# One decoder layer in fp32: the token mixer's weight loads issued from GpSimd's queue, and one statistics tile in another pool

## The chip, the cores and the metric

The kernel runs on one core of one Trainium2 chip. Its time is the device time of one execution in microseconds (us); lower is better. Times of several runs are given by their median. A profile is one execution recorded by the hardware profiler.

Short names used below: PE is TensorE (matmuls), PEld its weight loads, DVE VectorE, ACT ScalarE, POOL GpSimd, SP SyncE. SPq and POOLq are the sequencers of SP and POOL, which issue DMAs in the order of their programs.

## What is computed

One layer of a hybrid decoder on x of 2048 tokens by 1024 channels, in fp32: a token mixer and a gated feed-forward network, each on a modulated input and each followed by a LayerNorm.

```
u = x * (1 + scale) + shift                 # scale, shift, gate: rows of c @ w_ada
qa, ka, va, qb, kb, vb, ga, gb = split(u @ w_in)
ya = banded_attention(qa, ka, va, window 128, sinks)
yb = mixture of three dilated attentions (stride 1, 4, 16), merged by their denominators
y  = sigmoid(ga) * (ya @ w_a) + sigmoid(gb) * (yb @ w_b)
x  = LayerNorm(alpha * x + gate * (y @ w_o))
h  = silu(u2 @ w_gate) * (u2 @ w_up)         # u2: x modulated again
out = LayerNorm(alpha * x + gate2 * (h @ w_down))
```

## The kernel before

**Products.** Every fp32 operand of a large product is split into a high part and a rest (hi by ACT at L121, lo = src - hi by DVE at L122), and each product is three passes of matmuls over the parts: hi*hi, hi*lo, lo*hi.

**Weights.** `weights()` (L124) brings in one unit of weights of the token mixer: a tile `raw` of 128 x 1024 from the pool `raws` (3 buffers), one to four DMAs into it (L133), and the split into a tile `whl` (pool of 4 buffers), which PE reads. A DMA into a raw tile waits until the split of the tile that had this buffer before is done. The same pool of raw tiles serves the loads of `w_ada` in `ada_steps` (L197), which go on in the background. A unit has 24 matmuls of 512 columns on PE, one of the output stage (`w_a` and `w_b`, 768 columns) 18.

**Stages** (us from the start of the profile of before):
- 0 to 57, start-up: four groups of column pairs of `w_ada` (tile `pair`, L163) and of x (tile `xs`, L437), and four units of w_in (L431), are loaded by SP. DVE multiplies and adds the pairs (L172, L174) into `adc`, PE sums over the partitions (L183), DVE makes the scale and shift `mod` (L189), ACT the modulated input `ub` (L476) and its high part `ut`, and PE the first products (L418). PE, DVE and ACT follow an order written out by hand there. Of the four units' tiles three are the buffers of `raws`.
- 57 to 385: the dilated attention of stride 4 and 16, four residue classes; 385 to 823: four chunks of 512 tokens with the windowed attention and stride 1. The probabilities are transposed by DMA from SP (`pt`, L296) before the product with v. In both, the next stage's input is loaded by SP ahead (`xs`, L221; `ub`, L378).
- 823 to 1474: merging and output projection, chunks in the order 3, 0, 1, 2. `y_rows` (L900) loads each block of 128 tokens: `yl` (L908), `sty` (statistics, L909) and `xr` (L910); DVE and ACT make the merging weights (DVE L913 to L931, the exponentials on ACT at L917 and L932); PE transposes the merged rows (L953). ACT's sigmoids of the last gates ahead of it (L749) are stored to `s_s` (L750) and fetched later as `sg` (L990).
- 1474 to the end: gate and up with half of the multiplications of one level of Strassen (PE L1168), down (PE L1372), LayerNorms. `first_norm` (L1110) is here.

**What sets the order.** PE's order is that of the code (a manual schedule). On the other engines the order of instructions is set at compile time by a scheduler, by priorities: `weights()` has its priority raised by `PREFETCH` (100), so that its loads stand well ahead of their use. At run time every engine runs its program in order and waits on semaphores; an instruction that waits holds all that stands behind it on its engine, DMA issues on SPq and POOLq among them. Nothing reorders a queue at run time.

POOL has little to do before: three tables of distances (L251), casts of k (L605), an inverse square root per block (L772) and four stores of the normed input (`n_s`, L1049).

Of the kernel before, what the change touches and what calls it, by code (L numbers as in the profile page):

```python
# [12 lines left out]
F32 = mybir.dt.float32  # L13
# [44 lines left out]
def trunk(ctx, tc, x, c, w_ada, b_ada, w_in, sinks, w_a, w_b, w_o, ln1_g, ln1_b,  # L58
          w_gate, w_up, w_down, ln2_g, ln2_b, out):
    nc = tc.nc  # L60

    def dr(src, off, ap):
        return bass.AP(tensor=src.tensor, offset=src.offset + off, ap=ap)
# [56 lines left out]
    def split(hi, lo, src):  # L120
        nc.scalar.activation(hi, src, AF.Copy)  # L121
        nc.vector.tensor_tensor(lo, src, hi.bitcast(F32), op=OP.subtract)  # L122

    def weights(pieces, n=1024, by=None, offset=PREFETCH, into=None):  # L124


        with tc.high_priority(offset=offset):
            raw = raws.tile([128, 1024], F32, name="raw")
            o = 0
            for p in pieces:  # L130
                ap, m = p[:2]
                dst = p[2](raw) if len(p) > 2 else raw[:, o:o + m]
                nc.sync.dma_start(dst, ap)  # L133
                o += m
            whl = None if into else whls.tile([128, 2, 1024], F32R, name="whl")
            if by is not None:
                nc.vector.tensor_tensor(raw, raw, by, op=OP.mult)
            for i, (hi, lo) in enumerate(into or ()):
                split(hi, lo, raw[:, i * 512:(i + 1) * 512])
            if into is None:  # L140
                split(whl[:, 0, :n], whl[:, 1, :n], raw[:, :n])
        return whl
# [254 lines left out]
    def gate(us, c0):  # L397

        whl = weights([unit(c0)])
        ps = psum.tile([128, 512], F32, name="mm")  # L400
        dense(ps, KT, wT(whl), lambda k, b: us[k][b])
        return ps
# [4 lines left out]
    with ExitStack() as ph:  # L407
# [85 lines left out]
        def pool(name, bufs, stack=ph):  # L493
            return stack.enter_context(tc.tile_pool(name=name, bufs=bufs, reuse_waits="tile"))
# [46 lines left out]
        def project(us, pieces, outs, order, ps=None):  # L541
            if later is not None and ps is None:
                next(later, None)
            if ps is None:
                whl = weights(pieces)
                ps = psum.tile([128, 512], F32, name="mm")
                dense(ps, KT, wT(whl), lambda k, b: us[k][b])
            if order == 3:
                src = ps.rearrange("p (i a) -> p a i", a=4)
                hi, lo = (t.rearrange("p (a i) -> p a i", a=4) for t in outs)  # L550
            else:
                src, (hi, lo) = ps, outs
            with tc.high_priority(offset=EVICT):
                split(hi, lo, src)
            if nxt is not None:
                nxt.ahead(2)
            at.tick(5.2)

        def project_v(us, pieces_of, n, kper, lhs_of):
            ps = [psum.tile([128, 512], F32, name="mm") for _ in range(4)]  # L560
            for u0 in range(KT // kper):
                whl = weights(pieces_of(u0), kper * n)
                for t in range(4):
                    for kk in range(kper):
                        k = u0 * kper + kk
                        for i, (a, b) in enumerate(PASS):
                            nc.tensor.matmul(ps[t][:, :n], lhs_of(us[k][a], t),  # L567
                                             whl[:, b, kk * n:(kk + 1) * n],
                                             start=k == 0 and i == 0,
                                             stop=k == KT - 1 and i == 2)  # L570
                    if t % 2:
                        at.tick(2 * kper * n * 3 / 2400)
            return ps
# [193 lines left out]
    def layer_norm(pool, y, st, g, b, stats_only=False):  # L767
        mv = pool.tile([128, 2], F32, name="mv")
        rs = pool.tile([128, 1], F32, name="rs")
        nc.vector.bn_aggr(mv, st)  # L770
        nc.vector.tensor_scalar(rs, mv[:, 1:2], EPS, None, op0=OP.add)
        nc.gpsimd.tensor_tensor(rs, rs, mhalf, op=OP.pow)  # L772
        if not stats_only:
            scale_add(y, mv, g, rs, b)
        return mv, rs
# [27 lines left out]
    def x1t():  # L803
        return gp.tile([128, 4, 512], F32, name="x1t")
# [82 lines left out]
    with ExitStack() as ph:  # L887
# [5 lines left out]
        tmp = pool("tmp3", 2, ph)  # L893
# [166 lines left out]
    with ExitStack() as ph:  # L1060
        pool = partial(tile_pool, tc)
        w8 = pool("w8", 4, ph)
        tmp = pool("tmp4", 5, ph)
# [4 lines left out]
        lnp = pool("lnp", 2, ph)  # L1068
# [41 lines left out]
        def first_norm(l1, b):  # L1110

            t = x1t().rearrange("p a n -> p (a n)").rearrange("p (b n) -> p b n", b=2)
            nc.sync.dma_start(t, dr(n_s, b * 128 * D, [[D, 128], [128 * D, 2], [1, D]]))
            for i in range(2):
                st = tmp.tile([128, 2, 6], F32, name="st", bufs=2)
                for h in range(2):
                    nc.vector.bn_stats(st[:, h], t[:, i, h * 512:(h + 1) * 512])
                layer_norm(lnp, t[:, i], st, l1[:, :D], l1[:, D:])
            nc.sync.dma_start(dr(x1_s, (1024 + b * 128) * D, [[D, 128], [128 * D, 2], [1, D]]), t)
# [198 lines left out]
        for n, (p, g, w) in enumerate(sets):  # L1318
# [10 lines left out]
            if n in (1, 2):  # L1329
                hook(then, 7, partial(first_norm, l1, 2 * n - 2))  # L1330
# [31 lines left out]
    with ExitStack() as ph:  # L1362
# [3 lines left out]
        tmp = pool("tmp5", 2, ph)  # L1366
# [144 lines left out]
```

## Time and profile before

| | |
|---|---|
| time, median of 3 runs | 2775.33 us (2774.93 to 2778.13) |
| time of the profiled execution | 2777.24 us |
| its span, first to last instruction | 2775.5 us |
| PE busy | 2701.5 us (97%) |
| DVE, ACT, POOL busy | 69%, 43%, 2% |
| DMA queues | q1 (hardware): 503.06 MB, 61.2% of 16 engines; q0 (software): 2.10 MB, 0.2% |
| mean granted TensorE clock | 0.991 |

The profiled execution took 1.74 us more than its span. PE is busy for all but 74 us of the span, so a change of the time shows either in the holes of PE or in its granted clock. Of the two queues the hardware one holds the DMAs that SP issues, and the software one those that POOL issues (the four stores of L1049).

### The profile page before, as it was taken

The numbers are of one execution on the slowest core, as the hardware profiler recorded it, in microseconds if no ns is written. First come the engines' busy times: TensorE is split into PE (matmuls) and PEld (weight loads), VectorE is DVE, ScalarE is ACT, GpSimd is POOL, SyncE is SP. The second block draws the span as 40 slices with busy tenths as digits, with TensorE's granted clock in tenths as the row PEclk, the third lists the DMA queues.
The fourth block names the chain that finished last, engine by engine and source line by source line (L and its number), as shares of the span: only waits on it lengthen the run. The fifth ranks groups of instructions, "written<-read, shape, count | busy, mean of one in ns | idle before, by whom it ended". The sixth has DMA issues, their size and how long they took to land.

```text
span 2775.5 us, 36388 instructions
## 1 busy us (share of the span) xinstructions
PE 2701.5 (97%) x13331; PEld 2215.2 (80%) x13331; DVE 1918.9 (69%) x3506; ACT 1199.6 (43%) x1984; POOL 57.2 (2%) x63
## 2 busy tenths in 40 slices
PE   7999999999998999999999999998999999999998
PEld 5778778887887888888887888886888888888886
DVE  7766677788768867756458878767886666333387
ACT  3555565666594444343343333324222232432353
POOL 0000000000000000000000000000000000000011
PEclk9999999999999999999999999999999999999999
DMA  9966867776788476573545557725672334654463
GB/s 287 238 178 166 198 148 167 151 177 140 163 202 276 154 243 190 184 209 108 175 151 187 208 203 281 265 86 191 227 267 78 114 110 150 203 176 142 145 235 141
DMA packets 581332, 507.48 MB, mean 183 GB/s; under 512 B 207192, under 2 KB 467360, under 8 KB 581152
## 3 DMA queue, kind: packets, MB, share of 16 engines
q1 hardware_dynamic: 580576, 503.06, 61.2%
q8 instruction: 104, 1.70, 0.3%
q0 software_dynamic: 576, 2.10, 0.2%
q14 instruction: 76, 0.62, 0.1%
HBM read 341.67 MB, written 127.48 MB: 169 GB/s over the span
## 4 chain that ended last, share of the span: by engine, by line
PE 66%; DVE 4%; DMA 4%; ACT 1%; issue 1%; POOL 0%; SPq 0%; DVEq 0%; ACTq 0%; POOLq 0%
PE mm L1168 29%; PE mm L154 16%; PE acc L1372 14%; PE mm L1037 2%; PE o L1037 1%; PE s L1037 1%; PE o L306 1%; DMA x1t<-xT_s 1%; DMA x1t<-l_s 1%; PE s L271 1%; DMA sg<-s_s 1%; PE mm L567 1%; DVE cb L122 1%; DVE w L122 0%; ACT x1t L826 0%
## 5 line engine op out<-in xcount | busy, mean ns | idle before, releaser
L1168 PE MATMUL mm<-cb,w 128*128 128x512 f32 x3696 | 859.1, 394 | 9.9 <-ACT cb L121 3.2
L1168 PEld LDWEIGHTS mm<-cb,w 128*128 128x128 f32 x3696 | 693.8, 188 | 174.3 <-ACT w L121 5.4
L154 PE MATMUL mm<-ut,whl 128*128 128x512 f32 x3072 | 733.9, 395 | 10.1 <-DVE ut L122 5.1
L154 PEld LDWEIGHTS mm<-ut,whl 128*128 128x128 f32 x3072 | 572.2, 189 | 140.3 <-DVE ut L122 10.9
L1372 PE MATMUL acc<-hw 128*128 128x512 f32 x1848 | 419.1, 389 | 0.0
L1372 PEld LDWEIGHTS acc<-hw 128*128 128x128 f32 x1848 | 347.0, 188 | 71.9
L122 DVE TENSOR_TENSOR whl<-raw,whl 128x1024 fp32r<-128x1024 f32 (+1 forms) x228 | 265.2, 1164 | 145.8 <-ACT whl L121 145.6
L121 ACT ACTIVATE whl<-raw 128x1024 fp32r<-128x1024 f32 (+1 forms) x228 | 230.1, 1010 | 294.5 <-issue 69.0
L121 ACT ACTIVATE w<-g 128x1024 fp32r<-128x1024 f32 (+1 forms) x176 | 166.8, 951 | 387.6 <-PE mm L1168 318.7
L122 DVE TENSOR_TENSOR hw<-raw,hw 128x1536 fp32r<-128x1536 f32 x77 | 135.2, 1757 | 171.5 <-ACT hw L121 170.6
L121 ACT ACTIVATE hw<-raw 128x1536 fp32r<-128x1536 f32 x77 | 114.7, 1490 | 241.7 <-PE acc L1372 209.6
L122 DVE TENSOR_TENSOR w<-g,w 128x1024 fp32r<-128x1024 f32 (+1 forms) x176 | 191.1, 1087 | 39.2 <-ACT w L121 37.7
L294 DVE TENSOR_TENSOR ehl<-te,ehl 128x512 f16<-128x512 f32 (+1 forms) x160 | 98.3, 615 | 114.6 <-ACT ehl L293 114.4
L567 PE MATMUL mm<-whl,ut 128*128 128x512 f32 (+1 forms) x768 | 160.3, 365 | 0.0
L567 PEld LDWEIGHTS mm<-whl,ut 128*128 128x128 f32 x768 | 137.4, 188 | 16.4
L154 PE MATMUL mm<-q,whl 128*128 128x512 f32 x576 | 137.3, 393 | 0.8 <-DVE q L122 0.4
L154 PEld LDWEIGHTS mm<-q,whl 128*128 128x128 f32 x576 | 109.0, 190 | 24.9 <-DVE q L122 0.8
L1172 DVE TENSOR_TENSOR t<-mm,t 128x512 f32<-128x512 f32 x138 | 94.6, 687 | 48.5 <-PE mm L1168 48.0
L283 DVE CUSTOM_DVE_ANT_0 te<-s,tab 128x256 f32<-128x256 f32 (+1 forms) x320 | 109.6, 381 | 2.2 <-PE s L271 2.0
L306 PE MATMUL o<-v,pt 128*128 128x192 bf16 x1096 | 92.4, 236 | 4.8 <-DMA pt<-ehl 4.6
L306 PEld LDWEIGHTS <-pt 128*128 128x128 f16 x1096 | 75.6, 99 | 25.4 <-issue 18.3
L293 ACT ACTIVATE ehl<-te 128x512 f16<-128x512 f32 (+1 forms) x160 | 89.7, 561 | 12.0 <-DMA pt<-ehl 9.8
(195 smaller groups left out, 2606.5 us busy)
## 6 DMA issues: line engine op xcount, KB each, us to landing
raw<-in_w_in_dram SPq DMA_DIRECT2D x132, 512.0 KB, 4.3
raw<-h_s SPq DMA_DIRECT2D x77, 512.0 KB, 3.9
g<-in_w_gate_dram SPq DMA_DIRECT2D x22, 1024.0 KB, 5.3
g<-in_w_up_dram SPq DMA_DIRECT2D x22, 1024.0 KB, 5.3
h_s<-g SPq DMA_DIRECT2D x22, 1024.0 KB, 5.6
t_s<-x1t SPq DMA_DIRECT2D x22, 1024.0 KB, 5.1
raw<-t_s SPq DMA_DIRECT2D x77, 256.0 KB, 4.0
h_s<-g SPq DMA_DIRECT2D x22, 768.0 KB, 5.3
```

Of the source, the lines that this page charges most:

```text
L121: nc.scalar.activation(hi, src, AF.Copy)
L122: nc.vector.tensor_tensor(lo, src, hi.bitcast(F32), op=OP.subtract)
L154: nc.tensor.matmul(ps, lhs(k, a), rhs(k, b), start=i == 0, stop=i == n - 1)
L283: nc.vector.tensor_tensor_reduce(out=te[:, h, :nk], in0=ps[h], in1=tables[h][:, 256 - nk:], scale=1.0, scalar=-3e38, op0=OP.add, op1=OP.ma ...
L293: nc.scalar.activation(eh[:, 0], te[:, :, :nk], AF.Copy)
L294: nc.vector.tensor_tensor(eh[:, 1], te[:, :, :nk], eh[:, 0], op=OP.subtract)
L306: nc.tensor.matmul(pv[:, h, a:], pt[:, (a * 2 + h) * nb + j], v[:, :3 - a], start=j == 0 and a == 0, stop=j == nb - 1 and a == 1)
L567: nc.tensor.matmul(ps[t][:, :n], lhs_of(us[k][a], t), whl[:, b, kk * n:(kk + 1) * n], start=k == 0 and i == 0, stop=k == KT - 1 and i == 2)
L1037: nc.tensor.matmul(pss[b], mT[k][a][:, b * 128:(b + 1) * 128], whl[:, bb, kk * 512:(kk + 1) * 512], start=k == 0 and i == 0, stop=k == KT ...
L1168: nc.tensor.matmul(ps, r.of(m, k, a), us[k][b][:, LEFT[m]], start=first and k == 0 and i == 0, stop=last and k == 3 and i == 2, skip_group ...
L1172: nc.vector.tensor_tensor(out, ps, other, op=op)
L1372: nc.tensor.matmul(ps, hw[:, a, t * 128:(t + 1) * 128], hw[:, b, 1024:], start=first and i == 0, stop=last and i == 2, skip_group_check=True)
```

## The change

One line in `weights()` makes POOL issue the loads of the mixer's weights (w_in behind the first four units, w_a, w_b, w_o) instead of SP; what is loaded, into which buffers, stays. One line in `first_norm` takes its small tile `st` from the pool `lnp`, where it had been one of two buffers of the pool `tmp`.

```diff
@@ weights()
                 dst = p[2](raw) if len(p) > 2 else raw[:, o:o + m]
-                nc.sync.dma_start(dst, ap)
+                nc.gpsimd.dma_start(dst, ap)
                 o += m
@@ first_norm()
-                st = tmp.tile([128, 2, 6], F32, name="st", bufs=2)
+                st = lnp.tile([128, 2, 6], F32, name="st")
```

The programs of the engines show what this moves. First POOL, at the start of the program, before the change (L82 and L83 make the identity matrix; a row with xN is N instructions in succession):

```order
L82 MEMSET ident 128x128
L83 ISA
L83 AFFINE_SELECT ident<-ident 128x128
L251 IOTA ub 128x256 x3
L605 CAST k<-k 128x128 x18
L772 TENSOR_TENSOR rs<-rs,mhalf 128x1 x12
L1049 DMA n_s<-xr 128x1024 x4
```

And POOL at the same place with the change:

```order
L82 MEMSET ident 128x128
L83 ISA
L83 AFFINE_SELECT ident<-ident 128x128
L133 DMA raw<-in_w_in_dram 128x2x512 x3
L251 IOTA ub 128x256
L133 DMA raw<-in_w_in_dram 128x2x512
L133 DMA raw<-in_w_in_dram 128x8x128 x8
L133 DMA raw<-in_w_in_dram 128x2x512 x4
```

Three loads are now the first DMAs of POOL's program, with nothing ahead of them there but the identity matrix; all later loads, the casts of k and the square roots stand in one line behind them.

The same place on SP, as a difference; the rows of u_s (L480) are stores of the modulated input in the start-up, those of xs (L221) loads for the next stage:

```order
 L480 DMA u_s<-ub 128x512 x6
-L133 DMA raw<-in_w_in_dram 128x2x512 x2
+L221 DMA xs<-in_x_dram 128x4x128
 L480 DMA u_s<-ub 128x512
-L133 DMA raw<-in_w_in_dram 128x2x512
+L221 DMA xs<-in_x_dram 128x4x128
 L480 DMA u_s<-ub 128x512
```

Before, these first weight loads stood behind six of the eight stores, which wait for the start-up's results; on POOL they stand behind none of them.

The second place is SP between the attention and the output projection (855 to 863 us in the profile of before), where the blocks of chunk 0 are fetched for merging (sty, xr) and the gates stored (s_s). Before:

```order
L909 DMA sty<-st_s 128x40
L910 DMA xr<-o_s 128x512
L133 DMA raw<-in_w_a_dram 128x4x128
L133 DMA raw<-in_w_b_dram 128x2x128
L909 DMA sty<-st_s 128x40
L910 DMA xr<-o_s 128x512
L750 DMA s_s<-ub 128x512
L910 DMA xr<-o_s 128x512
L133 DMA raw<-in_w_a_dram 128x4x128
L133 DMA raw<-in_w_b_dram 128x2x128
L909 DMA sty<-st_s 128x40 x2
```

With the change:

```order
L750 DMA s_s<-ub 128x512
L910 DMA xr<-o_s 128x512
L909 DMA sty<-st_s 128x40
L750 DMA s_s<-ub 128x512
L909 DMA sty<-st_s 128x40 x2
L750 DMA s_s<-ub 128x512
L910 DMA xr<-o_s 128x512
L909 DMA sty<-st_s 128x40
L378 DMA ub<-u_s 128x4x128 x3
L750 DMA s_s<-ub 128x512
```

The loads of statistics stand behind the stores of gates only, no longer behind loads that wait for a weight buffer. ACT's program follows at this place: the last sigmoids of L749 alternate with one or two exponentials (L917, L932) where two sigmoids came in succession before, and ACT has 46 table loads in the whole program instead of 42, each where it passes between the two functions.

PE's program is the same but for one group of transposes in the first chunk of the output projection, and the instructions of gate, up and down stand in the same order on every engine.

## Rows read from the trace of the kernel before

**Rows 1.** The page: the span, and PE's busy time

```profile
span 2775.5 us, 36388 instructions
PE 2701.5 (97%) x13331; PEld 2215.2 (80%) x13331; DVE 1918.9 (69%) x3506; ACT 1199.6 (43%) x1984; POOL 57.2 (2%) x63
```

**Rows 2.** Waits of PE: line, released by; us in total, times, longest

```profile
PE mm L225 <- DMA xs<-in_x_dram: 10.0, 5, 3.8
...
PE mm L418 <- ACT ut L121: 7.0, 2, 3.7
...
PE o L306 <- DMA pt<-ehl: 4.6, 3, 1.7
...
PE mm L953 <- ACT ub L749: 3.1, 1, 3.1
```

**Rows 3.** Waits of SP's queue: the loads of weights, for their buffer

```profile
SPq L133 <- DVE whl L122: 276.4, 102, 7.2
```

**Rows 4.** Line L133: who waited for its transfers (us, times)

```profile
  ACT whl L121: 36.9, 16
```

**Rows 5.** Timeline in the attention: start, us, engine, line, operation [idle before]

```profile
189.50 5.79 PE L154 MATMUL mm<-ut,whl 128*128 128x512 f32 x24
...
331.61 0.38 SPq L133 DMA_DIRECT2D raw<-in_w_in_dram  x1
...
347.78 1.06 ACT L121 ACTIVATE whl<-raw 128x1024 fp32r<-128x1024 f32 x1 [5.04 <-PE mm L567]
```

**Rows 6.** Timeline of the start-up, all engines

```profile
19.69 1.23 DVE L122 TENSOR_TENSOR whl<-raw,whl 128x1024 fp32r<-128x1024 f32 x1 [0.26 <-ACT whl L121]
...
30.77 0.35 DVE L172 TENSOR_SCALAR adc<-pair,cols 128x256 f32<-128x256 f32 x1 [1.16 <-DMA pair<-in_w_ada_dram]
...
32.15 0.78 ACT L476 ACTIVATE ub<-s,mod 128x512 f32<-128x512 f32 x1 [10.22 <-DVE mod L189]
...
33.64 1.52 PE L418 MATMUL mm<-ut,whl 128*128 128x512 f32 x2 [3.67 <-ACT ut L121]
...
43.73 0.96 SPq L133 DMA_DIRECT2D raw<-in_w_in_dram  x2
```

**Rows 7.** Windows, start-up: busy time of each engine, PEclk, DMA share, GB/s

```profile
20.00:30.00 10.00, 9.54 (x39) 7.53 (x37) 9.26 (x20) 1.90 (x3) 0.00 (x0) 1.00 1.12 338
30.00:40.00 10.00, 6.36 (x22) 4.90 (x23) 8.71 (x23) 2.71 (x4) 0.00 (x0) 0.66 1.12 339
```

**Rows 8.** Timeline between attention and output projection, all engines

```profile
855.07 0.38 SPq L133 DMA_DIRECT2D raw<-in_w_a_dram  x1
856.05 0.46 SPq L909 DMA_DIRECT2D sty<-st_s  x1
...
859.58 0.17 DVE L913 TENSOR_TENSOR sm<-sty,nsk 128x8 f32<-128x8 f32 x1 [1.88 <-DMA sty<-st_s]
...
860.65 1.28 ACT L749 ACT_TABLE_LOAD   x1
...
862.60 0.66 PE L953 MATMUL mm<-ident,yl 128*128 128x128 f32 x4 [3.11 <-ACT ub L749]
864.96 1.12 PE L953 MATMUL mm<-ident,yl 128*128 128x128 f32 x4 [1.71 <-DVE q L122]
```

**Rows 9.** Windows, same columns as rows 7, of this place

```profile
858.00:874.00 16.00, 10.40 (x44) 7.92 (x43) 12.30 (x44) 8.38 (x16) 0.00 (x0) 0.79 0.92 298
```

**Rows 10.** Timeline of SP and PE around one wait for xs

```profile
186.12 0.40 SPq L133 DMA_DIRECT2D raw<-in_w_in_dram  x1
187.41 2.70 SPq L296 DMA_TRANSPOSE pt<-ehl  x2
...
192.97 0.44 SPq L221 DMA_DIRECT2D xs<-in_x_dram  x1
...
198.36 0.63 PE L225 MATMUL mm<-ident,xs 128*128 128x128 f32 x4 [2.64 <-DMA xs<-in_x_dram]
```

**Rows 11.** Line L1049, the DMAs that POOL issues: ns min/median/max, and landing

```profile
L1049 POOL DMA_DIRECT2D n_s<-xr x4: 533/536/746, 1472.2 to 1476.2; - x4
...
DMA to landing us min/median/max: 3.1/3.4/3.7
```

**Rows 12.** POOL's square roots: busy us, mean ns, idle before

```profile
L772 POOL TENSOR_TENSOR rs<-rs,mhalf 128x1 f32<-128x1 f32 x17 | 24.2, 1428 | 705.6 <-DVE rs L771 674.7 <-issue 30.7
```

## The prediction, made before the changed kernel ran

> **What bounds the kernel now.** I read the page first. PE is busy for 2701.5 of 2775.5 us [rows 1], so 74 us of holes, and the stretches at half clock that follow some of them, are all that a change of queues can win without shortening a matmul. Next I read PE's waits: who ended each hole [rows 2]. The reader is to look for the raw weights, or their split whl, and to miss them: PE's holes are put down to x tiles, modulated inputs, transposed probabilities and a sigmoid, of which no line is over 10.0 us. Third, SP's queue [rows 3]: there the loads of weights waited 276.4 us in 102 waits for a free buffer. That is large and looks like the prize, but it is the loads' own wait; it costs only what stands behind it on SP and is late for that reason. Fourth, the reverse: who waited for these loads [rows 4]: ACT, 36.9 us, and ACT is not full. In the attention a load issued at 331.61 is split at 347.78, three units later, and the split then waits for PE, not for the load [rows 5]. With 16 us of lead, an earlier load gives PE nothing. So the change must be judged at the few places where something else stood behind a weight load on SP, or where the loads now go at another time. The last views are timelines at the start-up and at the passage to the output projection, with windows for clock and DMA.
>
> **1. Start-up: three loads go out much earlier, +6.3.** Before, the first loads of L133 are issued at 43.73 [rows 6], behind the stores of the start-up. On POOL only the buffer holds them: the three raw tiles come free with the splits of the start-up's weights, of which the third begins at 19.69 and lasts 1.23, so all three are free by 20.9. From there 3 x 512 KB = 1.57 MB are moved in a stretch in which the DMA engines have no room: their share is 1.12 from 20 to 30 and from 30 to 40, at 338 and 339 GB/s [rows 7]. 1.57 MB at 339 GB/s are 4.6 us. What waits for DMA there is the path: DVE waits for a pair until 30.77, makes mod, ACT starts at 32.15 after 10.22 us without work, PE at 33.64 after 3.67 [rows 6]. DVE, ACT and PE keep a written order there, so nothing can be put in the hole. If the three loads delay the pair by their whole time, this hole grows by 4.6. The clock falls behind it already: 0.66 granted over 10 us is 6.8 us at the lower level (1.2 of 2.4 GHz), 3.4 us lost [rows 7]; a longer hole may lose half as much again, 1.7. Bounds: 0, if the pairs keep their rate, and 4.6 + 3.4 = 8.0 with a second whole stretch. I take +6.3, since rows 7 show no spare DMA time. Nothing is won back: after the start-up PE does not wait for weights.
>
> Here a rule speaks against the change. The rows show one stream of loads filling the DMA engines at 339 GB/s [rows 7]. The Trainium skill, page "DMA: Bandwidth & Descriptors", section "Issuing engines are not separate DMA queues", says that DMAs of SP, ACT and POOL run on the same 16 engines and interleave, and that issuing from several saves only issue time. By that rule the term is the +4.6 of shared bytes with its clock; if a second queue brought capacity of its own, it would be 0. No run here shows two queues at once.
>
> **2. Passage to the output projection, -4.0.** At 855.07 SP issues a weight load for which it had waited, and only at 856.05 the load of sty behind it; DVE gets sty at 859.58 after 1.88 us, ACT loads its table for the sigmoid at 860.65, behind the exponentials of that block, and PE goes on at 862.60 after 3.11 [rows 8]. With the change nothing that waits for a weight buffer stands ahead of sty; the stores of gates do, and they wait for sigmoids that PE feeds every 5.79 us [rows 5], which leaves a landing of some 3 us its time. So the hole of 3.11 can go. The next, 1.71 for DVE's part of q, belongs to the start of the stage and stays. Clock: 0.79 over 16 us is 6.7 us at the lower level, 3.4 lost [rows 9]; I count half, 1.7. Against that stand four more table loads on ACT, 1.28 each [rows 8], of which ACT's idle time takes most; I charge 0.8. Sum -3.1 - 1.7 + 0.8 = -4.0. Bounds: -6.5 (hole and whole clock loss gone) and +2.6 (two table loads on the path and the hole still there).
>
> **3. Attention: xs and pt, -1.5.** Typical is the hole at 198.36: its xs is issued at 192.97 behind two transposes of 2.70 us, and the weight load ahead of these, at 186.12, takes 0.40 [rows 10]. Taking out 0.4 at each of the three largest holes for xs gives -1.2, and 0.3 more for the three waits for pt. Bounds: -14.6, all of 10.0 and 4.6 [rows 2], if these transfers were late because they queued behind weights; +5, if the scheduler's new order of ACT and DVE opens as many holes as it closes.
>
> **4. POOL's queue, +0.5.** POOL now does all loads in order, and they wait for buffers. Behind them stand the casts of k and the square roots (1.43 us each [rows 12]). One of the latter is held for up to 2 us where the chunk's norm needs it; I charge 0.5, bounds 0 and 2. What a load costs POOL no row shows for these shapes. The nearest: a store of 128 rows of 4 KB takes 0.533 us and lands in 3.4 [rows 11]. A unit of w_in has 8 x 128 = 1024 rows of 512 B: between 0.533, if the cost is by instruction, and 8 x 0.533 = 4.3, if it is by row. PE takes 5.79 for a unit [rows 5], so both ends hide, at 16 us of lead. The shift of SP's own issue time (0.38 us each [rows 5]) frees SP, which is not the bound.
>
> **5. The tile st, 0.** Both pools have two buffers for it, the instructions are the same and nobody waits there.
>
> **Sum.** +6.3 - 4.0 - 1.5 + 0.5 = +1.3 on the profiled execution's 2777.24 gives 2778.5. That one lies 1.9 above the median of the runs, so I put the same +1.3 on 2775.33: 2776.6. A measurement of this kernel tells 0.2% (5.6 us) from no change.
>
> **Rivals.**
> *A, xs and pt were late because of the queue, faster.* In one queue a transfer waits for the 512 KB ahead of it. For it: SP's loads wait 276.4 us [rows 3], and xs and pt are small. Against it: in rows 10 the weight load is 6.8 us ahead of xs. If two thirds of the 14.6 go, term 3 is -9.7 and the whole +6.3 - 4.0 - 9.7 + 0.5 = -6.9: 2768.4. It decides from a term 3 of -8.4.
> *B, POOL's issue becomes the bound, slower.* If a row costs more than the 4.2 ns of rows 11 (0.533 over 128), a unit of 2048 rows (the windowed queries, 16 of them, two loads of 64 columns for 8 x 128 rows each) takes over 8.5 us where PE takes 5.79: 2.7 us each. Four in succession are 10.8, just under the lead of 16; at twice the price, 17 a unit, they are 45 less 16 = 29 per chunk, over four chunks 116. The point from which it decides is some 6.5 ns a row (13.3 - 5.79 = 7.5 a unit, four of them 30, less 16 = 14 per chunk). At that point 56 us are lost: 2832; a slight case, one chunk, gives about 2790. Against it: the one row of POOL's DMAs is far below.
> The Trainium skill, "SBUF — State Buffer", section "SBUF: two separate sides", warns that POOL cannot write descriptors while DVE runs certain fast copies. That would act as B does; no row here shows a DMA of POOL held in this way.
> *C, the start-up at its upper bound and no gain later, slower.* With term 1 at +8.0, term 2 at 0 and term 3 at 0, the sum is +8.5: 2783.8. For it: the written order, and that table loads are added just where term 2 expects its gain.
> *D, the loads are in effect unchanged.* If POOL's first loads are held up by POOL itself, term 1 is 0, and terms 2 to 4 give -5.0: 2770.3, within 0.2%. Against it: nothing stands ahead of them in POOL's program.
>
> **How the numbers follow.** My forecast, terms 1 to 4 near their values: 0.34, predicted time 2776.5, own range 2771 to 2781. D 0.10, which is counted half as no change and half as faster. A 0.20, C 0.24, B 0.12. Faster: A 0.20 and 0.05 of D, 0.25. Slower: B and C, 0.36. Same: 0.39. The range reaches down over most of A, to 2767, and up over C and the slight case of B, to 2791; outside are the far part of B (0.08), the bottom of A (0.06), and 0.04 for what I do not see.
>
> **What would show it.** Step 1: the hole of PE before L418 at some 38 instead of 33.64, the wait for a pair ahead of it longer than 1.16, the first loads of L133 at 17 to 21. Step 2: PE's wait for L749 gone from its list, sty issued right behind a store. Step 3: xs and pt still in the list with like sums. Step 4: casts and roots later but nobody waiting for them; L133's duration on POOL per load, which settles B. Wrong I would be if the pairs land as before although the DMA engines are full, if PE waits for whl, or if the new order on ACT and DVE opens holes of several us where the trace of before has none.

## The result, and the profile after

| | median | runs | ratio to the kernel before |
|---|---|---|---|
| before | 2775.13 us | 4 (2771.96 to 2778.13) | |
| changed | 2806.18 us | 4 (2803.07 to 2808.05) | 1.0104 [1.0091, 1.0117] |

The change costs 31 us; I had forecast no difference that can be told (2776.5, range 2767 to 2791). The profiled execution took 2808.05 us with a span of 2806.3. Its page, the lines that answer to rows 1, and the two DMA queues:

```profile
span 2806.3 us, 36596 instructions
PE 2706.8 (96%) x13331; PEld 2227.3 (79%) x13331; DVE 1923.7 (69%) x3506; ACT 1203.4 (43%) x1988; POOL 300.7 (11%) x383
...
q1 hardware_dynamic: 382944, 391.89, 46.2%
q0 software_dynamic: 32832, 113.27, 13.8%
```

POOL's software queue now moves 113 MB. PE is idle for 2806.3 - 2706.8 = 99.5 us, 25.5 more than before. Its waits, against rows 2 (line, released by; us in total, times, longest):

```profile
PE o L306 <- DMA pt<-ehl: 18.1, 11, 3.6
PE mm L225 <- DMA xs<-in_x_dram: 12.7, 6, 4.8
PE s L448 <- DMA xs<-in_x_dram: 12.2, 3, 8.4
PE mm L418 <- ACT ut L121: 6.6, 2, 3.4
...
PE mm L953 <- ACT ub L749: 2.7, 1, 2.7
...
PE mm L1037 <- ACT sg L992: 2.1, 2, 1.9
```

Rows 2 leave out one line of the kernel before, the second largest, which belongs beside these:

```profile
PE s L448 <- DMA xs<-in_x_dram: 8.5, 1, 8.5
```

The wait for the transposed probabilities has gone from 4.6 us to 18.1, those for xs (L225 and L448) grew by 6.4 together, and the wait for L749, which I had expected to go, is still 2.7. The first two are 19.9 of the 25.5. PE is also busy 5.3 us longer, although the group of L1168 alone takes 11.3 less (shown below): the matmuls elsewhere were slower, which the granted clock accounts for (see the attention, term 3). Between the first L567 and the first L953 of PE (60.5 and 897.4 in the changed kernel, 56.8 and 858.0 before, from the timelines) 35.7 us are lost; the start-up before it loses 3.7, and the output projection behind it takes 0.4 less than it had. Then something I had not looked for: gate and up take 8.1 us less (first L1168 to first L1372: 1513.7 to 2375.2, before 1474.7 to 2344.3).

### The profile page after: what moved, and what is told of

Same layout as the page of the kernel before. It is cut to its first block, busy times and chain, and to the rows that moved or that the text cites. A ratio compares the mean times of both kernels' runs of the same rounds, so it can differ in the third digit from the quotient of the medians.

```text
span 2806.3 us, 36596 instructions
## 1 busy us (share of the span) xinstructions
PE 2706.8 (96%) x13331; PEld 2227.3 (79%) x13331; DVE 1923.7 (69%) x3506; ACT 1203.4 (43%) x1988; POOL 300.7 (11%) x383
## 4 chain that ended last, share of the span: by engine, by line
PE 59%; DVE 7%; DMA 6%; issue 2%; ACT 2%; POOL 0%; SPq 0%; DVEq 0%; ACTq 0%; POOLq 0%
PE mm L1168 26%; PE acc L1372 14%; PE mm L154 13%; PE mm L1037 1%; DMA x1t<-xT_s 1%; DMA pt<-ehl 1%; PE o L1037 1%; PE s L1037 1%; DVE whl L122 1%; DMA x1t<-l_s 1%; PE o L306 1%; DVE w L122 1%; PE s L271 1%; DMA sg<-s_s 1%; DVE cb L122 0%
## 5 line engine op out<-in xcount | busy, mean ns | idle before, releaser
L1168 PE MATMUL mm<-cb,w 128*128 128x512 f32 x3696 | 847.8, 391 | 12.4 <-ACT cb L121 3.3
L1168 PEld LDWEIGHTS mm<-cb,w 128*128 128x128 f32 x3696 | 694.6, 188 | 164.8 <-ACT w L121 6.0
L154 PE MATMUL mm<-ut,whl 128*128 128x512 f32 x3072 | 741.0, 398 | 9.6 <-DVE ut L122 5.6
L154 PEld LDWEIGHTS mm<-ut,whl 128*128 128x128 f32 x3072 | 577.8, 191 | 141.7 <-DVE ut L122 11.4
L1372 PE MATMUL acc<-hw 128*128 128x512 f32 x1848 | 419.1, 389 | 0.0
L1372 PEld LDWEIGHTS acc<-hw 128*128 128x128 f32 x1848 | 346.9, 188 | 72.1
L133 POOL DMA_DIRECT2D raw<-in_w_in_dram x224 | 174.9, 783 | 906.3 <-DVE whl L122 377.9
L567 PE MATMUL mm<-whl,ut 128*128 128x512 f32 (+1 forms) x768 | 160.9, 366 | 1.3 <-DVE k L122 0.9
L567 PEld LDWEIGHTS mm<-whl,ut 128*128 128x128 f32 x768 | 137.3, 188 | 18.5 <-DVE k L122 1.4
L1414 POOL TENSOR_TENSOR rw<-rw,mhalf 128x1 f32<-128x1 f32 x15 | 22.0, 1465 | 1193.5 <-DVE rw L1413 1193.5
L154 PE MATMUL mm<-q,whl 128*128 128x512 f32 x576 | 136.1, 392 | 0.2 <-DVE q L122 0.2
L154 PEld LDWEIGHTS mm<-q,whl 128*128 128x128 f32 x576 | 108.8, 189 | 23.3 <-DVE q L122 0.6
L306 PE MATMUL o<-v,pt 128*128 128x192 bf16 x1096 | 96.6, 241 | 18.2 <-DMA pt<-ehl 18.1
```

The source lines that it names most:

```text
L133: nc.gpsimd.dma_start(dst, ap)
L154: nc.tensor.matmul(ps, lhs(k, a), rhs(k, b), start=i == 0, stop=i == n - 1)
L306: nc.tensor.matmul(pv[:, h, a:], pt[:, (a * 2 + h) * nb + j], v[:, :3 - a], start=j == 0 and a == 0, stop=j == nb - 1 and a == 1)
L567: nc.tensor.matmul(ps[t][:, :n], lhs_of(us[k][a], t), whl[:, b, kk * n:(kk + 1) * n], start=k == 0 and i == 0, stop=k == KT - 1 and i == 2)
L1168: nc.tensor.matmul(ps, r.of(m, k, a), us[k][b][:, LEFT[m]], start=first and k == 0 and i == 0, stop=last and k == 3 and i == 2, skip_group ...
L1372: nc.tensor.matmul(ps, hw[:, a, t * 128:(t + 1) * 128], hw[:, b, 1024:], start=first and i == 0, stop=last and i == 2, skip_group_check=True)
```

## The experiments

All are compared with the kernel before on the same chip; on the four chips used its median was 2776.0 to 2776.8. The first three deal with the edit of `st`, the next three with the place of the loss, then come its cause and two attempts at a better kernel.

### The edit of st alone

```diff
-                st = tmp.tile([128, 2, 6], F32, name="st", bufs=2)
+                st = lnp.tile([128, 2, 6], F32, name="st")
```

> The kernel before with the second edit alone (st in the pool lnp). Theory 1 (my step 5: the edit is nothing): 2775, within 3 us of before, and gate and up (PE L1168, 859.1 us busy in the profile before, 847.8 in the changed one) stay near 859. Theory 2 (the edit moves buffers and with that the speed of gate and up, which gave back 8.7 us in the changed kernel): 2766 to 2768, L1168 near 848.

Measured: 2765.71 us, ratio 0.9964 [0.9952, 0.9976]: 10.3 us faster. Theory 2. The kernel before, the changed one and this one, the group of L1168 in each page (busy us, mean ns of one):

```profile
L1168 PE MATMUL mm<-cb,w 128*128 128x512 f32 x3696 | 859.1, 394 | 9.9 <-ACT cb L121 3.2
```
```profile
L1168 PE MATMUL mm<-cb,w 128*128 128x512 f32 x3696 | 847.8, 391 | 12.4 <-ACT cb L121 3.3
```
```profile
L1168 PE MATMUL mm<-cb,w 128*128 128x512 f32 x3696 | 845.9, 390 | 9.5 <-ACT cb L121 3.2
```

One instruction after another costs 3 to 4 ns less, without one being left out. PE's timeline in the same stretch, before and with this edit, shows the pace (start, us, count):

```profile
1799.73 30.59 PE L1168 MATMUL mm<-cb,w 128*128 128x512 f32 x132
```
```profile
1799.80 30.54 PE L1168 MATMUL mm<-cb,w 128*128 128x512 f32 x134
```

30.59 / 132 is 231.7 ns, 30.54 / 134 is 227.9. The tile that a matmul streams through the array (its moving rows) lies in one of two pools, comb1 or comb2, 1848 matmuls each. Taking st out of the pool tmp moves all that stands behind it, comb2 among it, by 128 bytes in every partition, from 60672 to 60544; comb1 stays where it is. With the edit the time from one start to the next is 227 ns in both pools. Before, a pattern of twelve matmuls repeats through the stage, six of comb1 and six of comb2, with medians of 232, 232, 231, 227, 227, 227 and 234, 224, 237, 229, 237, 229 ns. So comb2's are slow, 232 in the median of all 1848, and with them the three of comb1 that follow them, though their own address did not change; the other half of comb1's takes 227 in both kernels. The twelve add up to 2766 ns instead of 2724, which over 3696 matmuls is 12.9 us; the whole stage (first L1168 to first L1372) goes from 869.7 to 857.2 us. The gain of 10.3, 6.7 to 13.3 by its interval, agrees.

The section on the kernel before said that the time can change only by the holes of PE or by its granted clock. Here is a third way: the pace of the matmuls themselves.

So the weights' own share of the change is not 31 us but about 40 (2806.2 - 2765.7 = 40.5 by the medians, 1.0104 - 0.9964 or 38.9 by the ratios).

### The address, put back and moved on

Both kernels have the edit of st; the new tile is never used.

```diff
-        tmp = pool("tmp4", 5, ph)
+        tmp = pool("tmp4", 5, ph); pool("tpad", 1, ph).tile([128, 32], F32, name="tpad")   # 64 in the second
```

> The second edit alone (st in lnp), with an unused tile of 128 bytes a partition in the pool tmp, so that comb2 and the pools behind it stand again at the addresses that they have in the kernel before (comb2 at 60672). Theory A (the gain of the edit of st is in the address of comb2's tiles): 2774 to 2778 again, matmuls of L1168 that read comb2 at 232 ns instead of 227. Theory B (the gain comes from the order or from st's buffer): 2764 to 2768, all at 227.

> The second edit alone with an unused tile of 256 bytes a partition in the pool tmp: comb2 at 60800, 256 above its address with the edit alone (60544, 227 ns a matmul) and 128 above that of before (60672, 232 ns). Theory A (the matmul is slow where the address of its moving rows is a multiple of 256, and not where it is 128 over one): 227 ns, 2764 to 2768. Theory B (it is slow from 60672 upwards, by what lies beside it): 232 ns, 2774 to 2778.

Measured: with 128 bytes 2777.19 us, ratio 1.0000 [0.9991, 1.0009], comb2's matmuls at 232 ns in the median, and the pattern of twelve is back; with 256 bytes 2766.00 us, 0.9958 [0.9943, 0.9973], all at 227 ns. Theory A both times: order and buffer of st play no part. The stage is slow with comb2 at 60672, a multiple of 256, and not 128 below or above; of the pools that the padding moves, these matmuls read comb2 alone. That three of comb1's six are slow too is not explained by theory A. The pages have L1168 at 858.3 and 848.8 us.

### Where the weights' loss arises: start-up, attention, output projection

One diff with three conditions (`calls[1]` is set behind the attention); all have the edit of st, so they are to be read against 2765.71.

```diff
+    calls = [0, False]
...
+        calls[0] += 1
+        queue = nc.gpsimd if calls[0] <= 3 else nc.sync                      # start-up
+        queue = nc.gpsimd if calls[0] > 3 and not calls[1] else nc.sync      # attention
+        queue = nc.gpsimd if calls[1] else nc.sync                           # projection
...
-                nc.sync.dma_start(dst, ap)
+                queue.dma_start(dst, ap)
...
+    calls[1] = True
```

> Only the first three loads of the mixer's weights go through POOL's queue, all others stay on SP (with the edit of st). Theory A (shared bytes in the full start-up): +5 to +7 on before, PE's L567 of the start-up 5.5 us later, as in the changed kernel; 2780 to 2782 if st is nothing. Theory B (the start-up recovers behind, or the 5.5 us came from another engine's new order): within 2 us of before.

> POOL issues the weight loads of the attention only; the first three and all of the output projection are on SP (with the edit of st). Theory A (transposes pt land later beside POOL's loads; this is most of the loss): +22 to +30 on before, PE's wait for pt again 14 to 20 us. Theory B (the loss comes from the three starts and follows by chance of phase): +0 to +6, PE's wait for pt near the 4.6 of before.

> POOL issues the weight loads of the output projection only, those of the attention are on SP (with the edit of st). Theory A (my term 2, sty no longer behind a load that waits): -2 to -5 on before, the wait for L749 gone. Theory B (the table loads and late weights eat it): 0 to +3.

| on POOL | median | ratio to before | over the edit of st alone |
|---|---|---|---|
| first three loads | 2768.03 | 0.9973 [0.9963, 0.9982] | +2.3 |
| attention | 2791.94 | 1.0061 [1.0049, 1.0074] | +26.2 |
| output projection | 2771.50 | 0.9986 [0.9977, 0.9995] | +5.8 |
| all (the change) | 2806.18 | 1.0104 [1.0091, 1.0117] | +40.5 |

The three expectations were written against the kernel before, which lacks the gain of st; their times are off by that gain, and only the last column tells the loss. The attention has two thirds of it, with PE's wait for pt at 17.2 us (11 times) as theory A has it, though its time, 15.9 over before, is under the 22 that I had written. The sum of the three is 34.3; the other 6 are not assigned, and each row is uncertain by some 3 to 4. In the profiles the stretch of the attention is 30.0 us longer in its own run than with the edit of st alone, and 38.4 in the changed kernel. My start-up is right in place and too large at the end: PE's first L567 stands at 61.7, 4 us behind the one with the edit alone (57.7), and some of that is won back later. The output projection, where I had expected a gain, loses. What PE waits for there begins with ACT (timelines of POOL, ACT and PE, without the lines in between):

```profile
1202.11 0.92 POOL L133 DMA_DIRECT2D raw<-in_w_in_dram  x1 [10.54 <-DVE whl L122]
1206.89 0.88 POOL L133 DMA_DIRECT2D raw<-in_w_in_dram  x1 [3.86 <-DVE adacc L201]
...
1207.87 1.06 ACT L121 ACTIVATE whl<-raw 128x1024 fp32r<-128x1024 f32 x1 [10.20 <-DMA raw<-in_w_in_dram]
...
1213.61 0.21 ACT L932 ACTIVATE sb<-sb 128x12 f32<-128x12 f32 x1 [1.89 <-DVE sb L931]
1213.84 1.28 ACT L992 ACT_TABLE_LOAD   x1
...
1215.78 0.50 PE L154 MATMUL mm<-ut,whl 128*128 128x512 f32 x1 [1.33 <-ACT sg L992]
```

ACT stands 10.20 us at a split whose load is late: POOL issued it at 1202.11, after 10.54 us of waiting for a buffer, and it landed at 1207.77. The next load then waits for a tile of w_ada (adacc). The sigmoid behind the split (L992) is late, also by a wait for DVE's sb and two table loads, and PE waits for the sigmoid.

### A quarter of the bytes

```diff
-                ap, m = p[:2]
-                dst = p[2](raw) if len(p) > 2 else raw[:, o:o + m]
+                ap, m = light(p[0]), p[1] // 4        # light: a quarter of the columns
+                dst = p[2](raw)[:, :2] if len(p) > 2 else raw[:, o:o + m]
...
-                split(whl[:, 0, :n], whl[:, 1, :n], raw[:, :n])
+                split(*[whl[:, i, :n].rearrange("p (r c) -> p r c", r=4) for i in range(2)], raw[:, None, :n // 4].to_broadcast([128, 4, n // 4]))
```

> The changed kernel with a quarter of the weights' bytes: each load brings a quarter of its columns, and the split reads that quarter four times, so that the weights are not the reference's; number, place and length of all other instructions stay, and through the attention every engine's program is that of the changed kernel. Theory A (the transposes pt land later because POOL's loads are in flight beside them): PE's wait for pt falls from 18.1 us to under 6, the holes for xs from 12.7 to under 8, and the time to 2765 to 2778. Theory B (it is the new order of ACT's and DVE's programs): the wait for pt stays at 14 to 20 us and the time above 2790.

This kernel leaves out three quarters of each weight, so its output is not the layer's. Measured: 2761.87 us, ratio 0.9938 [0.9920, 0.9956]; lower still than I had written. PE's waits:

```profile
PE mm L225 <- DMA xs<-in_x_dram: 6.6, 5, 2.7
...
PE o L306 <- DMA pt<-ehl: 5.9, 6, 1.7
```

From the first transpose of probabilities to the last every engine's program is that of the changed kernel, and as many loads go out at the same places; the loss is gone with the bytes. The transposes land in 3.41 us on average instead of 3.91, and 3 of 97 take over 5 us instead of 22. The scheduler's new order, my theory B, is not the cause, nor is POOL's issuing as such.

### Loads cut in four, and ACT's queue in place of POOL's

```diff
-                nc.gpsimd.dma_start(dst, ap)
+                cut(dst, ap)          # four DMAs, each a quarter of the columns
```

> The changed kernel with most loads of POOL cut in four DMAs, so that a packet is 1024 bytes instead of 4096, with the same bytes in all. Theory A (one turn of a 4096 byte packet, 223 ns, holds back SP's small packets): PE's wait for pt falls from 18.1 to under 9 us, the time to 2785 to 2798. Theory B (what counts is that the load's bytes move at the same time as the transpose, in whatever packets): wait for pt 14 to 22 us, time 2800 to 2820 (POOL issues four times as often, 2 to 3 us a unit, still under PE's 5.8).

Measured: 2808.52 us, ratio 1.0113 [1.0100, 1.0127]; PE's wait for pt 15.4 us in 12. The time is theory B's. But the trace has the same 27648 packets of 4096 bytes as the changed kernel, so the size of a packet, which I had meant to change, did not change, and the run says nothing of it. The other hardware queue does:

```diff
-                nc.gpsimd.dma_start(dst, ap)
+                nc.scalar.dma_start(dst, ap)
```

> The changed kernel with ACT's queue in POOL's place for the weights (a hardware queue, as SP's, whose packets of weights are 512 and 256 bytes; ACT waits itself where a buffer is not yet free, so its own work may be late). Read from it is the flight of the transposes beside weight loads. Theory A (what delays them is a second queue of any kind that moves weights at the same time): transposes take 3.9 us or more on average from issue to landing, over 15 of them more than 5 us, PE's wait for pt 12 us or more. Theory B (it is the software queue with packets of 4096 bytes, that take 223 ns a turn): 3.7 us or less on average, as in the kernel before (3.65), under 13 above 5 us, PE's wait for pt under 8. Time: open, 2770 to 2830.

Measured: 2792.64 us, ratio 1.0057 [1.0040, 1.0074]. Its weights are for the most part packets of 512 bytes (143360 of them) and 256. PE waits for pt 13.5 us in 9; of the transposes whose landing the trace has, the mean flight is 3.92 us and 19 of 106 take over 5. Theory A: a second queue of another kind does it too. The time is not to be read further, since ACT here also waits for buffers itself.

### w_ada on POOL's queue as well

```diff
-                nc.sync.dma_start(raw, dr(w_ada, k * 128 * 6 * D + v * D, [[6 * D, 128], [1, D]]))
+                (nc.gpsimd if calls[1] else nc.sync).dma_start(raw, dr(w_ada, k * 128 * 6 * D + v * D, [[6 * D, 128], [1, D]]))
```

> POOL issues the loads of weights and of w_ada (L197) in the output projection, SP those of the attention. Theory A (with POOL for the weights alone, loads for the same three raw tiles stand in two queues, and a weight load waits for a w_ada tile whose own load SP issues late, so ACT waits 8 to 10 us for a weight and PE for ACT's sigmoid): the wait of L1037 and L154 for ACT sg (2.2 and 1.3 us) goes, the time falls from 2771.5 to 2764 to 2768. Theory B (weights from POOL are late there in any case): 2770 to 2774, the waits stay.

This stands on the kernel with the output projection's weights on POOL. Measured: 2774.03 us, 0.9993 [0.9982, 1.0005]. Of the two named waits of PE for sg one is gone and the other is 0.5 us instead of 2.2, but the time is not lower: theory A falls, and theory B, which has the time, expected these waits to stay. ACT's waits for late weights are as large as with the weights alone on POOL (88.9 us against 89.9, and 41.2 with the edit of st alone). From issue to landing a weight load of this stage takes 4.9 us on average from POOL and 4.1 from SP in the kernel with 256 bytes of padding.

### Small loads on POOL instead

```diff
-                nc.sync.dma_start(st, st_s[rows, :])     # sty; in the other kernel: dma_start(xs, src)
+                nc.gpsimd.dma_start(st, st_s[rows, :])
```

> The second edit alone, and of all loads only the 16 of sty (20 KB each, L909) on POOL's queue, the weights on SP: the change turned round, the small late load leaves the queue in which it waits. Theory A (my term 2 was right on the place, wrong on what to move): the wait of L953 for L749 goes, 2761 to 2764. Theory B (the hole belongs to the stage's start and to the table loads): 2764 to 2768, hole near 3.

> The second edit alone, and of all loads only those of xs for the next class (L221, 256 KB each) on POOL's queue. Theory A (xs waits on SP behind the transposes and stores; 8 MB in all do not crowd the transposes): PE's wait of L225 for xs falls from 7.1 us to under 4, wait for pt stays under 5, 2756 to 2763. Theory B (256 KB beside a transpose cost as the weights do): wait for pt above 8, 2766 to 2775.

Both have the edit of st. Measured: sty 2773.24 us, 0.9988 [0.9979, 0.9997]; xs 2768.57, 0.9965 [0.9954, 0.9976]. Both theories A fall by their times; with sty theory B does too, which had 2764 to 2768, and with xs theory B has the time but not the wait for pt (4.3 us, not over 8). With sty on POOL the waits at this place grow (L953 for L749 4.8 us, for DVE's yl 4.6). With xs there PE's wait of L225 falls from 7.1 us to 2.6, as written, but the wait of L154 for ut grows from 5.5 to 8.9, and the time is not lower than with the edit of st alone. That edit, at 2765.7, is the version that beats both kernels.

## Why the prediction was wrong

**Term 3, the attention: -1.5 forecast, about +26 measured. This is the step that failed.** It lies outside the bounds that I gave the term, -14.6 to +5. I had asked only how much sooner xs and pt would be issued, and taken what their transfers meet on the way as unchanged. Both halves can be read at one hole. Before, SP's queue at the hole in front of L306 at 676.97:

```profile
670.07 1.23 SPq L296 DMA_TRANSPOSE pt<-ehl  x1
671.35 0.67 SPq L133 DMA_DIRECT2D raw<-in_w_in_dram  x1
...
673.02 0.44 SPq L133 DMA_DIRECT2D raw<-in_w_in_dram  x1
673.57 1.23 SPq L296 DMA_TRANSPOSE pt<-ehl  x1
674.85 2.08 SPq L133 DMA_DIRECT2D raw<-in_w_in_dram  x4
```
```profile
676.97 0.73 PE L306 MATMUL o<-v,pt 128*128 128x192 bf16 x8 [1.68 <-DMA pt<-ehl]
```

The transpose at 673.57 was indeed held up (its ehl is begun at 671.20 and takes 0.69), and it lands in 3.35 us; four more loads go out only behind it. The same place with the change, POOL's queue, then SP's, DVE's and PE's:

```profile
696.32 4.35 POOL L133 DMA_DIRECT2D raw<-in_w_in_dram  x8 [12.82 <-ACT whl L121]
```
```profile
698.93 8.59 SPq L296 DMA_TRANSPOSE pt<-ehl  x3
```
```profile
698.16 0.69 DVE L294 TENSOR_TENSOR ehl<-te,ehl 128x512 f16<-128x512 f32 x1
```
```profile
704.78 1.25 PE L306 MATMUL o<-v,pt 128*128 128x192 bf16 x8 [2.54 <-DMA pt<-ehl]
```

The transpose is issued 0.08 us behind its ehl, 1.6 sooner than before: the relief of SP that the diff promises is real. But POOL has put eight loads out in 4.35 us when its buffers came free; they land from 699.3 to 705.0. The trace has no landing for the transpose among them, but PE's wait for it ends at 704.78, after 5.8 us instead of 3.35. SP's order had also been a pacing: the load behind a transpose could not start before it. Over all 160 transposes the wait from ehl to issue falls from 0.41 to 0.31 us on average. Over those whose landing is recorded the flight rises from 3.65 to 3.91, and those over 5 us from 12 of 100 to 22 of 97; in the three other traces with the same weight loads on SP (the edit of st alone and the two paddings) they are 9, 9 and 12. All of the 22 have a weight load in flight beside them. In the median the flight hardly differs (lines on L296, before and after; us to landing, min/median/max):

```profile
DMA to landing us min/median/max: 2.4/3.2/6.9
```
```profile
DMA to landing us min/median/max: 2.4/3.4/8.9
```

It is the long ones that PE meets. In the changed kernel PE waits over 0.3 us for pt ten times, and in seven of these the landing is recorded: those transposes flew 5.3 to 8.9 us, with one to eight weight loads in flight. The three holes of before ended with flights of 3.3 to 3.6, beside three or four weight loads of SP's own queue. The quarter of the bytes took the loss away, ACT's queue brought the flights and the wait for pt back, so this cause is shown for pt. That the growth of the xs waits (L225, 10.0 to 12.7 us) is of the same kind fits the quarter too (6.6), but was not tested by itself, and the three other traces with these loads on SP have 7.1, 5.5 and 6.4.

The holes are only half of the 35.7 us. Windows from the first L567 to the first L953, with the change and before, hold the same 4834 matmuls:

```profile
60.50:897.40 836.90, 794.50 (x4834) 652.33 (x4833) 587.28 (x1593) 499.28 (x1140) 141.54 (x201) 0.96 0.71 173
```
```profile
56.80:858.00 801.20, 777.35 (x4834) 640.18 (x4833) 580.11 (x1580) 494.93 (x1134) 7.69 (x20) 0.99 0.76 180
```

PE is idle for 42.4 us instead of 23.9 and busy for 17.2 us longer, at a granted clock of 0.96 instead of 0.99: it is at the lower level (1.2 of 2.4 GHz) for 61 us of this stretch with the change, for 17 before. The hole shown above is one of these places. Windows of the changed kernel around it, and of before around its own:

```profile
697.00:704.00 7.00, 5.25 (x29) 4.07 (x27) 4.16 (x14) 3.49 (x12) 3.56 (x7) 1.00 0.99 205
704.00:711.00 7.00, 6.22 (x28) 5.04 (x29) 4.81 (x15) 3.08 (x8) 1.43 (x3) 0.52 0.55 109
```
```profile
670.00:677.00 7.00, 5.32 (x30) 4.13 (x29) 4.19 (x14) 3.52 (x12) 0.00 (x0) 1.00 0.73 158
677.00:684.00 7.00, 7.00 (x44) 5.68 (x44) 4.70 (x15) 3.95 (x11) 0.00 (x0) 1.00 0.84 207
```

Behind the hole of 2.54 us the clock is at 0.52, behind that of 1.68 it stays at 1.00. That the longer holes are what lowers it was not tested by itself. The DMA engines are busy to 0.71 and 0.76 over the whole stretch, but to 0.99 in the 7 us in which this transpose is under way, and to 0.73 in those of before: a mean share with room left says nothing of what two transfers cost each other at the moment when PE waits. The Trainium skill, "DMA: Bandwidth & Descriptors", section "Issuing engines are not separate DMA queues", says that such transfers interleave on the same 16 engines. The trace agrees, with a weight load in flight beside each of the 22 long transposes, and I had used that rule in the start-up alone.

**Term 1, the start-up: +6.3 forecast; +2.3 in the median, +4 at the first L567.** The mechanism was right, three loads delaying the pairs and with them mod, and the size too large. Timeline after (POOL, then all engines):

```profile
17.13 0.93 POOL L133 DMA_DIRECT2D raw<-in_w_in_dram  x1 [15.78 <-DVE mod L189]
...
21.21 0.72 POOL L133 DMA_DIRECT2D raw<-in_w_in_dram  x1 [1.52 <-DVE whl L122]
```
```profile
28.57 0.48 DVE L174 SCALAR_TENSOR_TENSOR adc<-pair,cols,adc 128x256 f32<-128x256 f32 x1 [2.07 <-DMA pair<-in_w_ada_dram]
...
31.04 0.64 PE L448 MATMUL s<-ident,xs 128*128 128x128 f32 x4 [3.48 <-DMA xs<-in_x_dram]
...
37.69 3.65 PE L418 MATMUL mm<-ut,whl 128*128 128x512 f32 x7 [3.19 <-ACT ut L121]
```

The loads stand at 17 to 21, L418 at 37.69 (I wrote 38), 4.05 behind rows 6. The wait for pairs is spread over several instructions (4.9 us in all from 23 to 35, before 1.2), and the hole before L418 did not grow; a new one for xs came ahead of it. What was mis-sized is what follows: I let the delay stand to the end, and of the 4 us at the first L567 the median keeps 2.3.

**Term 2, the passage: -4.0 forecast, +5.8 for the output projection.** The +5.8 is from the run with this part alone; in the profile of the changed kernel the stretch takes 2.0 us more than with the edit of st alone (616.3 and 614.3), so its size within the change is uncertain. sty no longer stands behind a weight load, and PE's hole is 2.7 instead of 3.1, where the traces with these loads on SP have 2.0 to 3.2: the load behind which it stood was not what set it. The last sty is now issued behind gate stores at 899.88. I can name the place of the loss (ACT waiting for late weights), but the one cause that I tried, the mixing of two queues over the same three tiles, is not enough; the cause stays open.

**Term 4, POOL: +0.5.** Right as far as the trace shows: DVE waits 0.9 us in all for POOL's square roots, before 0.4, and nobody waits for the casts. A load of w_in costs POOL 0.88 us in the median (line L133, ns min/median/max), near the lower of my bounds 0.533 and 4.3, and rival B did not come; no load of POOL is over 1.19 us, with DVE busy 69% of the time. The case that the Trainium skill warns of ("SBUF — State Buffer", section "SBUF: two separate sides", as the prediction cites it) does not show in this trace.

```profile
L133 POOL DMA_DIRECT2D raw<-in_w_in_dram x224: 535/882/1187, 17.1 to 1431.8; - x112
```

**Term 5, st: 0 forecast, -10.3 measured.** I had compared instructions, buffers and waits, and not where the pools behind it come to lie. That the edit gained was luck, and it hid a quarter of what the weights cost. Without this gain the change would stand at some 2816, farther off.

**The rivals.** The slower side had 0.36, but for POOL's issue and the start-up. Rival A, that pt and xs would gain from a queue of their own, has the right two lines of the list and the wrong sign.

## What to carry to other kernels

A bulk load that is moved from a shared queue to a queue of its own starts as soon as its buffer is free, and here that was at times the moment at which PE waited for a small transfer: price the small transfer's flight among the bulk bytes, not only its earlier issue. Ask of an order that looks like a blockage what it keeps apart. When an edit moves a tile to another pool, look at the addresses of all pools behind it, and time it alone before it is put in one change with another.

## What was not expected of the hardware

Matmuls of 128x512 in fp32 took 232 ns from start to start, in the median of 1848, with the tiles of their moving rows at addresses that are multiples of 256 (the pool at 60672), and 227 ns at 128 below (60544) or above (60800). It holds in all fourteen kernels here: two have the pool at 60672, twelve at one of the others. In the two slow ones three of the six matmuls on the other pool, at an address that did not change, took 231 to 232 ns as well, so the rule is not simply one of a matmul's own moving rows. 128 bytes a partition were worth 10 us of 2776, a quarter of what moving 111 MB of loads to another queue cost. Why the address counts is open.
